# Two weight sums of the first seven-for-eight pair made early, and a second load buffer for up's second tiles

## The chip, the cores and the metric

One Trainium2 chip, of which the kernel uses one core. The core's engines are TensorE (PE; its weight loads are listed as PEld), VectorE (DVE), ScalarE (ACT), GpSimd (POOL) and SyncE (SP), which here only issues DMA transfers. The metric is the device time of one execution in microseconds (us), as the median of several runs.

## The reference

One layer of a hybrid decoder for 512 prompt tokens and 32 sample tokens (T = 544 columns), all in float32: a half-step FFN, a token mixer (differential attention beside an mLSTM), and a second half-step FFN. Only the two FFNs bear on the change:

```python
def half_ffn(x, g_pre, g_post, w_gate, w_up, w_down):
    h = rmsnorm(x, g_pre)
    u = jax.nn.silu(h @ w_gate) * (h @ w_up)
    return x + 0.5 * rmsnorm(u @ w_down, g_post)
```

`w_gate` and `w_up` are 1024 x 2816, `w_down` is 2816 x 1024. The FFN dimension is cut into KF = 22 tiles of 128, the model dimension into KT = 8 blocks of 128 (WK = 4 is half of them), and the columns into two halves of HALF = 272.

## The kernel before

**Precision.** A float32 product is made of three matmuls in a faster float format: each operand is split into a high and a low part, and high x high, high x low and low x high are added in PSUM. `parts` makes a split: ScalarE casts the high part (L240), VectorE subtracts it from the source (L241). Weight splits land in tiles `wh` and `wl`, three of each, and a new one waits until an old one's last matmul.

**Phases of an FFN.** `ffn` runs twice (li = 0, then li = 1 after the mixer).

1. *Plain tiles*, m = 0 to 3 (PLAIN = 4). For each tile and column half, `gate` and `upper` are 24 matmuls each (L252 to L254). The norm's factor `rstd` isn't applied to the input but to the result, by VectorE on reading PSUM (L561 for gate, L575 for up); so the first products can run before the sums of squares are ready. Tiles 0 and 1 are written out at the head of `ffn`, and `lead_out` reads out the first results once `rstd` is there. Tiles 2 and 3 are a list of eight jobs (`jobs`), of which the last three are left for later (`beside`).
2. *Seven-for-eight pairs*, m = 4 to 21, two at a time. Strassen's scheme: the model dimension is halved and the columns are halved, and seven products instead of eight are made of sums of weight blocks and sums of input blocks. The input sums ("factors", tiles `t` and `h8`) are made once by the generator `right_parts`: VectorE scales X (L423), combines quarters and splits each. The weight sums are made by `quadrants` for each pair. With g0, g1 and u0, u1 the upper and lower halves of gate's and up's weights, product 7 uses s3 = g0 + u0, product 5 uses u0 + u1, product 6 adds g0 to that, and product 3 adds g1. All four sums are VectorE adds of 128 x 1024 (L490, the helper `plus`). In order, the products are 1, 5, 6, 2, 7, 3, 4; each is 2 x 12 matmuls (L474 to L476). During the first pair, the rest of the factors and the three left jobs are made between the products.
3. *The down projection*, `down`.

**Weights.** SP loads them. `ffn_weights` yields the split plain tiles gate 0, up 0, gate 1, up 1 and so on; one load of 1 MB holds two neighbouring tiles. For m = 0 and 1 the two buffers of pool `raw` are loaded by `ffn_first`; for m = 2 and 3 gate's and up's loads take the same two buffers again, as they become free (L225). The pairs' weights come through the inner function `raws` (L648): the first pair's gate half lies in the not yet used part of tile `u`, its up half in tile `rawx`.

**Space.** Pools are stacked. In the first FFN, the pool `early` with tile `xt` (six blocks of 4 KB per partition) holds the input rows; after the transposes `bias_windows` uses block 0 (`oh`), block 1 (`rb`) and block 2 (`gsb`) for a small matmul (L961), a copy (L962) and a DMA out (L964). The pool of the `t` factors, three tiles of 8.5 KB, opened after that, begins where `early` began. In the second FFN it lies on tiles of the mixer that hold the last w_out weights (`wt2`). The pool `h8` has four tiles; the factors for products 2, 7, 3 and 4 take one each. The sum s3 lies in the first half of `X0`.

**Order.** The kernel is written against a layer that tracks which instruction uses which bytes, chooses among the ready instructions of an engine by planned times at build, and fixes the resulting order for each engine; a tile that is asked for while all buffers of its pool are in use waits. During the setup in the first FFN, TensorE's order is the written one, up to and with the matmul at L961. Each engine and each DMA queue takes its instructions in the fixed order.

Of the kernel before, what the change touches and what calls it, by code (L numbers as in the profile page):

```python
# [10 lines left out]
F32 = mybir.dt.float32  # L11
# [3 lines left out]
ALU = mybir.AluOpType  # L15
# [19 lines left out]
KT = D // 128  # L35
KF = FFN // 128
# [3 lines left out]
WK = 4  # L40
# [3 lines left out]
PLAIN = 4  # L44
# [160 lines left out]
class _Builder:  # L205
# [188 lines left out]

    def ffn_weights(self, li, first=None, skip=0):

        wg, wu, _ = self.ffn_views(li)
        for mc in range(KF // 2):
            cs = slice(mc * 256, mc * 256 + 256)
            if mc == 0:  # L400
                rg, ru = first or self.ffn_first(li)
            else:
                rg, ru = self.load_raw(wg[:, :, cs], 256), self.load_raw(wu[:, :, cs], 256)
            for sub in range(2):
                for r in (rg, ru):
                    if skip:
                        skip -= 1
                    else:
                        yield self.split(r, KT, sub * 128, step=KT)
# [66 lines left out]
            self.last_mm = nc.tensor.matmul(ps, lhsT=wl[:, k, cs], rhs=high, start=False, stop=sp,  # L476
                                            skip_group_check=True).ins

    def quadrants(self, loaded, raws, small, kept, put, beside, making):

        nc = self.nc
        flat = self.X.tiles[0].rearrange("p k t -> p (k t)")
        s3 = flat[:, 0:1024].rearrange("p (k m) -> p k m", k=WK)
        space = flat[:, 1024:1024 + 2 * T].rearrange("p (a t) -> p a t", a=2)
        C0, C1 = slice(0, HALF), slice(HALF, T)

        def plus(out, x, y):
            nc.vector.tensor_tensor(out=out, in0=x, in1=y, op=ALU.add)  # L490
        for u in range(PLAIN, KF, 2):
            (g0, g1), (u0, u1) = ((r[:, 0:WK], r[:, WK:KT]) for r in loaded)
            if PLAIN < u < KF - 2:
                loaded = raws(u + 2)
            uu = kept(u) if u < KEEP else space
            p1, p5, u2 = (small.tile([128, 2, HALF], F32, name=name) for name in ("p1", "p5", "u2"))
            a, b = [], []
            for p in PRODUCTS:
                if u == PLAIN:
                    next(making, None)  # L500
                    if p == 5:
                        loaded = raws(u + 2)

                if p == 5:
                    plus(s3, g0, u0)
                    plus(u0, u0, u1)
                elif p == 6:
                    plus(u0, u0, g0)
                elif p == 3:
                    plus(u0, u0, g1)  # L510
                src = {1: g0, 2: g1, 4: u1, 7: s3}.get(p, u0)
                w = [x.rearrange("p (k a) m -> p k (a m)", a=2) for x in self.w_tiles()]
                self.parts(src, *w)
                for r in range(2):
                    if p == 1:
                        a.append(self.acc.tile([128, 512], F32, name="acc")[:, 0:HALF])
                    elif p == 5:
                        b.append(self.ps_tile()[:, 0:HALF])
                    ps = b[r] if p in (5, 3) else self.smp.tile([128, 512], F32, name="smp")[:, 0:HALF] if p == 2 else a[r]
                    self.seven(ps, p, w, slice(r * 128, r * 128 + 128), p in (1, 5, 2), p in (2, 3, 4))  # L520
                    if p in (1, 5, 6):
                        nc.scalar.copy(out={1: p1, 5: p5, 6: u2}[p][:, r], in_=ps)
                    elif p == 2:
                        x = uu[:, r, C0]
                        plus(x, ps, p1[:, r])
                        nc.scalar.activation(out=x, in_=x, func=AF.Silu, scale=-1.0)
                    elif p == 7:
                        plus(uu[:, r, C1], ps, p5[:, r])
                    elif p == 3:
                        x = u2[:, r]  # L530
                        plus(x, ps, x)
                        nc.scalar.activation(out=x, in_=x, func=AF.Silu, scale=-1.0)
                    elif p == 4:
                        x = uu[:, r, C0]
                        nc.vector.tensor_tensor(out=x, in0=ps, in1=x, op=ALU.mult)
                    if u == PLAIN:
                        next(beside, None)
                if p == 3:
                    x = uu[:, :, C1]
                    nc.vector.tensor_tensor(out=x, in0=x, in1=u2, op=ALU.mult)  # L540
            if u >= KEEP:
                put(u, uu)

    def ffn(self, li, hs, ws, gpre, gpost, finish, before=None, u=None, lead=None, done=None):

        nc, tc = self.nc, self.tc
# [3 lines left out]
        def weight():  # L550
            return ready.pop(0) if ready else next(gen)
        with ExitStack() as ctx:
# [43 lines left out]
            if not lead:  # L596
                first = [self.mmh(p, x, hs, 0) for p, x in zip((pg, pu, pn), w)]
# [30 lines left out]
            xd = tc.dram_tile([128, KT, T], F32, name="x_ffn%d" % li)  # L628
            for k in range(0, KT, WK):
                nc.gpsimd.dma_start(out=xd[:, k:k + WK], in_=self.X[:, k:k + WK])  # L630
            factors = ctx.enter_context(tc.tile_pool(name="t%d" % li, bufs=3))

            place = own.tile([128, 2 * OWN, T], F32, name="u")
            making = self.right_parts(gpre, place, factors)
            more = tc.tile_pool(name="more%d" % li, bufs=1)
            small = more.__enter__()
            views = self.ffn_views(li)

            def raws(m):
                if m == PLAIN:  # L640
                    g = place[:, KT:2 * OWN].rearrange("p k t -> p (k t)")[:, 0:2048].rearrange("p (k m) -> p k m", k=KT)
                else:
                    g = self.raw.tile([128, 8, 256], F32, name="raw")
                u = self.X.tiles[1].rearrange("p k t -> p (k t)")[:, 0:2048].rearrange("p (k m) -> p k m", k=KT)
                if (m - PLAIN) % 4 == 0:
                    u = small.tile([128, 8, 256], F32, name="rawx")
                for r, w in zip((g, u), views):
                    nc.sync.dma_start(out=r, in_=w[:, :, m * 128:m * 128 + 256])  # L648
                return g, u
# [6 lines left out]
            for i, (f, m, half) in enumerate(jobs[:last]):  # L656
                if i % 4 == 0:
                    w = {gate: weight(), upper: weight()}
                if i == 0:
                    first = raws(PLAIN)  # L660
                f(m, half, w[f])
                upto = max(0, steps * (i + 1 - ahead) // (last - ahead))
                for _ in range(done, upto):
                    next(making)
                done = upto

            def beside():
                for f, m, half in jobs[last:]:
                    f(m, half, w[f])
                    yield  # L670
# [9 lines left out]
            def put(m, uu):  # L680
# [3 lines left out]
                s = self.own[:, i:i + 4].rearrange("p (a b) t -> p a b t", a=2)  # L684
                self.parts(uu, s[:, 0], s[:, 1])
                rows.update({m + a: (s[:, 0, a, :], s[:, 1, a, :]) for a in range(2)})
            self.quadrants(first, raws, small, kept, put, beside(), making)
            more.__exit__(None, None, None)
            self.down(li, ns, rows, factors, ctx.enter_context(tc.tile_pool(name="late%d" % li, bufs=2)), xd, gpost,
                      finish)  # L690
# [1292 lines left out]
```

## Time and profile before

| what | value |
|---|---|
| median of three runs (lowest to highest) | 1110.11 us (1108.96 to 1114.35) |
| the profiled execution, its own time | 1109.74 us |
| its span in the profile | 1107.9 us |
| mean granted TensorE clock | 0.999 |
| VectorE, ScalarE busy | 858.5 us, 641.0 us |
| DMA moved | 160.35 MB |

The profile is one execution on the chip. Its page gives the busy time of each engine, the span in 40 slices, the chain of work that ended last and the costliest groups of instructions. The trace behind it answers narrower questions: the timeline of an engine in a stretch (start, duration, engine, line, operation, what is written and read, how many rows were joined, and in brackets the idle time just before and what ended it), sums over stretches, who waited for whom (in total, how often, longest), and DMA issues with their time to landing. A tile's name stands without its number, so `acc` is any of three PSUM tiles.

The first FFN takes about the first 370 us, the second about the last 370; the plain tiles give way to the first pair at some 60 us and 767 us.

### The profile page before, as it was taken

The numbers are of one execution on the slowest core, as the hardware profiler recorded it, in microseconds if no ns is written. First come the engines' busy times: TensorE is split into PE (matmuls) and PEld (weight loads), VectorE is DVE, ScalarE is ACT, GpSimd is POOL, SyncE is SP. The second block draws the span as 40 slices with busy tenths as digits, with TensorE's granted clock in tenths as the row PEclk, the third lists the DMA queues.
The fourth block names the chain that finished last, engine by engine and source line by source line (L and its number), as shares of the span: only waits on it lengthen the run. The fifth ranks groups of instructions, "written<-read, shape, count | busy, mean of one in ns | idle before, by whom it ended". The sixth has DMA issues, their size and how long they took to land. (4 is left out here: it accounts for less than half of the span.)

```text
span 1107.9 us, 21556 instructions
## 1 busy us (share of the span) xinstructions
PE 1087.6 (98%) x8616; PEld 1048.7 (95%) x8616; DVE 858.5 (77%) x1636; ACT 641.0 (58%) x1292; POOL 155.1 (14%) x201
## 2 busy tenths in 40 slices
PE   8999999999999999999999999999999999999997
PEld 7999999999999998889889879999999999999997
DVE  5898787888577899658776477899987778957764
ACT  4655454565557657667564566774555455555664
POOL 0100000000110234421243541000000000012000
PEclk9999999999999999999999999999999999999999
DMA  9534233326995244643355645765233323299822
GB/s 262 192 123 148 77 114 94 98 83 190 225 221 182 65 142 136 197 125 91 86 165 173 180 143 184 212 212 173 90 97 97 112 79 104 68 273 208 187 98 82
DMA packets 145589, 160.35 MB, mean 145 GB/s; under 512 B 6013, under 2 KB 135397, under 8 KB 144208
## 3 DMA queue, kind: packets, MB, share of 16 engines
q1 hardware_dynamic: 115040, 99.11, 29.8%
q0 software_dynamic: 27472, 57.14, 21.0%
q10 hardware_dynamic: 2976, 2.71, 0.9%
q8 instruction: 68, 1.11, 0.4%
q14 instruction: 33, 0.27, 0.1%
HBM read 143.19 MB, written 16.28 MB: 144 GB/s over the span
## 5 line engine op out<-in xcount | busy, mean ns | idle before, releaser
L240 ACT CAST wh<-raw 128x512 fp32r<-128x512 f32 (+2 forms) x169 | 130.9, 800 | 100.8 <-PE acc L253 29.4
L241 DVE TENSOR_TENSOR wl<-raw,wh 128x512 fp32r<-128x512 f32 (+2 forms) x169 | 151.9, 912 | 46.7 <-ACT wh L240 46.0
L252 PE MATMUL acc<-h,wh 128*128 128x272 f32 x552 | 164.7, 298 | 0.0
L254 PE MATMUL acc<-h,wl 128*128 128x272 f32 x552 | 160.2, 291 | 0.0
L253 PE MATMUL acc<-h,wh 128*128 128x272 f32 x552 | 159.9, 290 | 0.0
L476 PE MATMUL acc<-t,wl 128*128 128x272 f32 x472 | 136.7, 290 | 1.4 <-DVE wl L241 1.4
L474 PE MATMUL acc<-t,wh 128*128 128x272 f32 x472 | 136.7, 290 | 0.0
L475 PE MATMUL acc<-t,wh 128*128 128x272 f32 x472 | 136.1, 289 | 0.0
L252 PEld LDWEIGHTS acc<-h,wh 128*128 128x128 f32 x552 | 104.0, 188 | 8.1 <-issue 7.5
L253 PEld LDWEIGHTS acc<-h,wh 128*128 128x128 f32 x552 | 104.1, 189 | 0.3 <-DVE y L1446 0.2
L254 PEld LDWEIGHTS acc<-h,wl 128*128 128x128 f32 x552 | 103.8, 188 | 0.6 <-issue 0.4
L474 PE MATMUL acc<-h,wh 128*128 128x272 f32 x360 | 104.2, 290 | 0.0
L476 PE MATMUL acc<-h,wl 128*128 128x272 f32 x360 | 104.2, 289 | 0.0
L475 PE MATMUL acc<-h,wh 128*128 128x272 f32 x360 | 103.6, 288 | 0.0
L241 DVE TENSOR_TENSOR wl<-X,wh 128x1024 fp32r<-128x1024 f32 x66 | 80.7, 1223 | 27.8 <-ACT wh L240 27.7
L240 ACT CAST wh<-X 128x1024 fp32r<-128x1024 f32 x66 | 69.3, 1050 | 40.7 <-PE aux L475 25.9
L476 PEld LDWEIGHTS acc<-t,wl 128*128 128x128 f32 x472 | 88.7, 188 | 1.8 <-DVE wl L241 1.7
L475 PEld LDWEIGHTS acc<-t,wh 128*128 128x128 f32 x472 | 89.0, 189 | 0.1
L474 PEld LDWEIGHTS acc<-t,wh 128*128 128x128 f32 x472 | 88.8, 188 | 0.0
L721 POOL DMA_DIRECT2D late<-in_ffn_w_down_dram x12 | 18.7, 1562 | 438.2 <-issue 376.4
L476 PE MATMUL aux<-h,wl 128*128 128x272 f32 x240 | 69.6, 290 | 0.0
L474 PE MATMUL aux<-h,wh 128*128 128x272 f32 x240 | 69.5, 289 | 0.0
(516 smaller groups left out, 3278.0 us busy)
## 6 DMA issues: line engine op xcount, KB each, us to landing
raw<-in_ffn_w_gate_dram SPq DMA_DIRECT2D x18, 1024.0 KB, 5.4
raw<-in_w_in_dram SPq DMA_DIRECT2D x28, 512.0 KB, 4.4
late<-in_ffn_w_down_dram POOLq DMA_DIRECT2D x12, 1024.0 KB, 9.9
rawx<-in_ffn_w_up_dram SPq DMA_DIRECT2D x10, 1024.0 KB, 5.5
X<-in_ffn_w_up_dram SPq DMA_DIRECT2D x8, 1024.0 KB, 5.5
raw<-in_ffn_w_down_dram SPq DMA_DIRECT2D x8, 1024.0 KB, 9.9
raw<-in_ffn_w_down_dram SPq DMA_DIRECT2D x10, 768.0 KB, 4.8
raw<-in_w_out_dram SPq DMA_DIRECT2D x7, 1024.0 KB, 5.5
```

The lines of the kernel that those rows point to most:

```text
L240: self.nc.scalar.copy(out=high, in_=src)
L241: self.nc.vector.tensor_tensor(out=low, in0=src, in1=high.bitcast(F32), op=ALU.subtract)
L252: nc.tensor.matmul(ps, lhsT=wh, rhs=xh(k0 + k), start=st, stop=False)
L253: nc.tensor.matmul(ps, lhsT=wh, rhs=xl(k0 + k), start=False, stop=False)
L254: self.last_mm = nc.tensor.matmul(ps, lhsT=wl, rhs=xh(k0 + k), start=False, stop=sp).ins
L474: nc.tensor.matmul(ps, lhsT=wh[:, k, cs], rhs=high, start=st, stop=False, skip_group_check=True)
L475: nc.tensor.matmul(ps, lhsT=wh[:, k, cs], rhs=low, start=False, stop=False, skip_group_check=True)
L476: self.last_mm = nc.tensor.matmul(ps, lhsT=wl[:, k, cs], rhs=high, start=False, stop=sp, skip_group_check=True).ins
L721: nc.gpsimd.dma_start(out=ts[j], in_=rows_of(a, j, up), accum_op=ALU.add)
```

## The change

Three edits, all in the two FFNs:

- **The first pair's two sums.** s3 = g0 + u0 and u0 + u1 of the first pair (m = 4) are written right after the pair's loads, before the first of the jobs of tiles 2 and 3, no longer inside `quadrants` at product 5. The first one's result lies in a tile of `h8` instead of `X0`. Later pairs make their sums as before.
- **Up's second tiles.** The load of up's tiles 2 and 3 goes into a tile of the pool of `t` factors (`self.spare`), no longer into the second buffer of `raw`.
- The loop of `ffn_weights` ends after the plain tiles; nothing asked for later ones.

```diff
     def ffn_weights(self, li, first=None, skip=0):
         wg, wu, _ = self.ffn_views(li)
-        for mc in range(KF // 2):
+        for mc in range(PLAIN // 2):
             cs = slice(mc * 256, mc * 256 + 256)
             if mc == 0:
                 rg, ru = first or self.ffn_first(li)
             else:
-                rg, ru = self.load_raw(wg[:, :, cs], 256), self.load_raw(wu[:, :, cs], 256)
+                rg = self.load_raw(wg[:, :, cs], 256)
+                ru = self.spare.tile([128, 8, 256], F32, name="t")
+                self.nc.sync.dma_start(out=ru, in_=wu[:, :, cs])
...
-    def quadrants(self, loaded, raws, small, kept, put, beside, making):
+    def quadrants(self, loaded, s3, raws, small, kept, put, beside, making):
...
         flat = self.X.tiles[0].rearrange("p k t -> p (k t)")
-        s3 = flat[:, 0:1024].rearrange("p (k m) -> p k m", k=WK)
...
-                if p == 5:
+                if p == 5 and u > PLAIN:
+                    s3 = flat[:, 0:1024].rearrange("p (k m) -> p k m", k=WK)
                     plus(s3, g0, u0)
                     plus(u0, u0, u1)
...
-            factors = ctx.enter_context(tc.tile_pool(name="t%d" % li, bufs=3))
+            self.spare = factors = ctx.enter_context(tc.tile_pool(name="t%d" % li, bufs=3))
...
                 if i == 0:
                     first = raws(PLAIN)
+                    s3 = self.h8.tile([128, WK, 256], F32, name="h8")
+                    for out, x in ((s3, first[0]), (first[1][:, 0:WK], first[1][:, WK:KT])):
+                        nc.vector.tensor_tensor(out=out, in0=x[:, 0:WK] if x is first[0] else x, in1=first[1][:, 0:WK],
+                                                op=ALU.add)
...
-            self.quadrants(first, raws, small, kept, put, beside(), making)
+            self.quadrants(first, s3, raws, small, kept, put, beside(), making)
```

## The prediction

> **What bounds the kernel now.** The page comes first: its span line and the line of busy times.
>
> ```profile
> span 1107.9 us, 21556 instructions
> PE 1087.6 (98%) x8616; PEld 1048.7 (95%) x8616; DVE 858.5 (77%) x1636; ACT 641.0 (58%) x1292; POOL 155.1 (14%) x201
> ```
>
> TensorE is busy for 1087.6 of 1107.9 us, so 20.3 us is all that any change can win that takes no matmul away, and this one takes none away. The profiled execution took 1109.74 us, 1.84 more than its span; the median of the three runs is 1110.11, so I work from 1109.74 and keep 0.4 us in mind. Next, the table of stretches around the first pair in each FFN (each stretch, its length, then busy time and instructions of PE, PEld, DVE, ACT, POOL, then clock, DMA share and GB/s).
>
> ```profile
> 20.00:46.00 26.00, 26.00 (x191) 23.87 (x190) 21.13 (x49) 18.93 (x42) 2.18 (x4) 1.00 0.72 242
> 46.00:91.00 45.00, 44.58 (x350) 43.99 (x350) 44.77 (x57) 22.63 (x31) 5.07 (x10) 1.00 0.49 153
> 744.00:769.00 25.00, 23.89 (x188) 23.59 (x187) 23.21 (x35) 14.62 (x22) 3.24 (x6) 1.00 0.55 177
> 769.00:800.00 31.00, 30.21 (x236) 29.91 (x237) 29.96 (x36) 15.49 (x23) 1.62 (x3) 1.00 0.41 134
> ```
>
> In the first FFN VectorE has 4.87 us to spare from 20 to 46 us and 0.23 from 46 to 91: there it is full. TensorE nevertheless loses only 0.42 there. In the second FFN TensorE loses 1.11 + 0.79 = 1.90 between 744 and 800, beside a VectorE that is idle for 1.79 and 1.04. So what can be won near the edit is 0.42 + 1.90 = 2.3 us. The waits of TensorE in these places, the first FFN's first:
>
> ```profile
> PE acc L252 <- DVE sqe L575: 0.4, 1, 0.4
> ```
> ```profile
> PE acc L476 <- DVE wl L241: 1.4, 1, 1.4
> PE acc L252 <- DVE sq L561: 0.4, 1, 0.4
> ```
>
> Three waits, all on VectorE: two for a PSUM tile that it reads out late, one for the low half of the first product's weights.
>
> **The change, part by part.** *The two sums.* VectorE's rows of the first pair, first FFN and then second:
>
> ```profile
> 64.04 1.20 DVE L490 TENSOR_TENSOR X<-u,rawx 128x1024 f32<-128x1024 f32 x1
> 65.17 1.27 DVE L241 TENSOR_TENSOR t<-u,t 128x1088 fp32r<-128x1088 f32 x1
> 66.37 0.42 DVE L575 TENSOR_TENSOR sqe<-acc,r 128x272 f32<-128x272 f32 x1
> 66.72 1.20 DVE L490 TENSOR_TENSOR rawx<-rawx 128x1024 f32<-128x1024 f32 x1
> ```
> ```profile
> 768.06 1.22 DVE L241 TENSOR_TENSOR wl<-u,wh 128x1024 fp32r<-128x1024 f32 x1
> 771.95 1.23 DVE L490 TENSOR_TENSOR X<-u,rawx 128x1024 f32<-128x1024 f32 x1
> 774.63 1.22 DVE L490 TENSOR_TENSOR rawx<-rawx 128x1024 f32<-128x1024 f32 x1
> ```
>
> The sums are these two L490 adds. Their count, size and operand memories stay; only their place moves, so 2 x 1.20 = 2.4 us of VectorE per FFN go from the full stretch to an earlier one. In the first FFN the reader at 66.37, for which TensorE waited 0.4, stands behind the 1.20 at 64.04: without it, it comes earlier than it is needed. What is late next is nothing that the waits show, so **-0.4**. In the second FFN the reader of the third wait comes after 774.63, behind both adds: **-0.4**. The wait of 1.4 ended with the split at 768.06, ahead of both old adds, so their removal does nothing for it.
>
> What the adds meet in their new place: they need the pair's weights. Issue and landing of `rawx`, first FFN and second:
>
> ```profile
> 21.42 0.58 SPq L648 DMA_DIRECT2D rawx<-in_ffn_w_up_dram  x1
> ```
> ```profile
> rawx<-in_ffn_w_up_dram SPq DMA_DIRECT2D x1, 1024.0 KB, 11.6
> ```
> ```profile
> 730.61 0.37 SPq L225 DMA_DIRECT2D raw<-in_ffn_w_gate_dram  x1
> 738.31 0.37 SPq L648 DMA_DIRECT2D rawx<-in_ffn_w_up_dram  x1
> 745.34 0.37 SPq L225 DMA_DIRECT2D raw<-in_ffn_w_up_dram  x1
> ```
> ```profile
> rawx<-in_ffn_w_up_dram SPq DMA_DIRECT2D x1, 1024.0 KB, 10.3
> ```
>
> First FFN: 21.42 + 11.6 = 33.0 us, ahead of the VectorE idle time in which the sums would fit:
>
> ```profile
> 40.27 0.79 DVE L567 TENSOR_TENSOR sq<-sq,sqe 128x272 f32<-128x272 f32 x2 [1.32 <-ACT sqe L566]
> ```
>
> One 1.20 fits into these 1.32; the other has room among the rest of the 4.87 idle us. Cost 0; if that cover were gone, at most 2 x 1.20 lands on the weight splits of that stretch. Second FFN: 738.31 + 10.3 = 748.6. The sums can't start before that, and from there VectorE is nearly full. Its one long gap:
>
> ```profile
> 752.88 1.22 DVE L241 TENSOR_TENSOR wl<-raw,wh 128x1024 fp32r<-128x1024 f32 x1 [1.49 <-ACT wh L240]
> ```
> ```profile
> 751.79 2.00 ACT L240 CAST wh<-raw 128x1024 fp32r<-128x1024 f32 x2 [2.27 <-DMA raw<-in_ffn_w_up_dram]
> ```
>
> That gap is a wait for up's second tile, issued at 745.34. With the tile in its new place the load needs no `raw` buffer and can go right behind the gate's at 730.61 (the buffer's former holder, the last w_out weights, is read by then), so the gap closes: VectorE has 2.4 us more to do before 769 and 1.49 us less to wait. The balance, +0.95, would fall on the 1.4 wait; at the other end, if the planner leaves the sums until after the split at 768.06, the closed gap takes that wait away. Range -1.45 to +0.95, taken as **0**, near the middle, since nothing tells the order.
>
> ```profile
> 738.53 0.55 POOL L630 DMA_DIRECT2D x_ffn<-X  x1 [4.08 <-DVE X L363]
> ```
>
> `rawx` took 10.3 us beside this save of X from another queue, against 5.5 for the load at 36.41 below. [...]
>
> *Up's second tile in the first FFN.* The new place is the first buffer of pool `t`, which lies where `early` was: its 8 KB per partition are blocks 0 and 1 of `xt`, which the bias windows use for `oh` and `rb` until their matmul at L961 (`gsb` lies in block 2). Rows of the old load and its split, and of TensorE:
>
> ```profile
> 36.41 0.37 SPq L225 DMA_DIRECT2D raw<-in_ffn_w_up_dram  x1
> ```
> ```profile
> raw<-in_ffn_w_up_dram SPq DMA_DIRECT2D x1, 1024.0 KB, 5.5
> ```
> ```profile
> 43.00 1.23 DVE L241 TENSOR_TENSOR wl<-raw,wh 128x1024 fp32r<-128x1024 f32 x1 [0.19 <-ACT wh L240]
> ```
> ```profile
> 44.09 0.81 PE L961 MATMUL aux<-xt 33*4 33x384 f32 x2
> 44.83 0.40 PE L252 MATMUL acc<-ha,wh 128*128 128x272 f32 x1
> ```
> ```profile
> 44.90:52.70 7.80, 7.80 (x62) 7.80 (x63) 7.80 (x14) 2.61 (x4) 2.89 (x5) 1.00 0.45 120
> ```
>
> The load can be issued at 44.09 + 0.81 = 44.90 instead of 36.41. It lands 5.5 later, 50.40; a cast of 1.0 (two took 2.00 above) and a subtract of 1.23 make the tile ready at 52.63. TensorE spaces its matmuls by 7.80/62 = 0.126 us, 24 to a product: gate of tile 2 runs 44.83 to 47.85, and the next product by the written order is up of tile 2. In that order TensorE would stand still for 52.63 - 47.85 = **4.8 us**. It need not be in that order, for the order on the engines isn't the written one:
>
> ```profile
> 60.19 0.29 PE L475 MATMUL acc<-t,wh 128*128 128x272 f32 x1
> 60.32 0.29 PE L252 MATMUL acc<-ha,wh 128*128 128x272 f32 x1
> ```
>
> `seven` writes its twelve matmuls in one run; here plain ones stand after the second, because the low half wasn't planned to be ready. A planner that knows the load to be late has gate of tile 2 for the other half and gate of tile 3 to put first, 2 x 3.02 us, which reaches 53.9 and covers 52.63. Between 0 and +4.8 I take **0**; the planner fixes the order before the run, so a load later than planned still stalls. On SP, later loads stand behind this one's wait. The next one before was this:
>
> ```profile
> 50.98 6.35 SPq L648 DMA_DIRECT2D raw<-in_ffn_w_gate_dram  x2
> ```
>
> It comes after 44.90, so nobody is late by that.
>
> *The factor's place.* The sum's `h8` tile is the fourth factor's buffer, so factor 4 must wait until product 7's weights are split off the sum:
>
> ```profile
> 78.92 1.22 DVE L241 TENSOR_TENSOR wl<-X,wh 128x1024 fp32r<-128x1024 f32 x1
> ```
> ```profile
> 79.04 1.11 ACT L240 CAST h<-u 128x1088 fp32r<-128x1088 f32 x1 [0.60 <-DVE u L448]
> ```
> ```profile
> 88.44 0.29 PE L474 MATMUL acc<-h,wh 128*128 128x272 f32 x1
> ```
>
> Split done at 80.14, cast 1.11, subtract 1.27: 82.5, and product 4 begins at 88.44. Nothing, with 5.9 us of cover; were the cover gone, the 1.1 us by which the cast moves. Likewise the third `t` factor now shares its place with up's tile, split before that factor is made. The shortened range of `ffn_weights` costs nothing, since nobody asked it for later tiles.
>
> **Sum.** -0.4 - 0.4 + 0 + 0 = -0.8: 1109.74 - 0.8 = 1108.9, and with half of the 0.4 by which the median lies higher, **1109.1 us**.
>
> **The rivals.** *Sums wait for their weights (second FFN).* If the planner believes `rawx` to land at the usual time, about 5.5 us after 738.31, it puts the sums at some 744 us, and VectorE, which works in order, stands until 748.6. Behind them stand the read-outs of PSUM and the splits; 2.4 us of sums then follow, and what VectorE lacks by 769 grows from 0.95 to some 3. For it: it stood 1.49 us at 752.88 for just such a misjudged load. Against it: the products ahead of the pair have some us of lead. Place 1111: 1109.74 - 0.8 + 0.95 to 3.
>
> *Up's tile late (first FFN), the slower side.* TensorE in the old order at 47.85 waits until 52.63: 1109.74 + 4.8 - 0.8 = 1113.7. It decides as soon as fewer than two other products (6.0 us) are put ahead. If the tile's place is kept until `gsb` is out as well, the load starts at 48.99 at the earliest:
>
> ```profile
> 48.99 0.74 POOL L967 DMA_DIRECT2D windows<-bias_row  x1 [1.29 <-DMA bias_row<-xt]
> ```
>
> 48.99 + 5.5 + 2.23 = 56.7, a stall of 8.9, and 1117.8. For it: the load moves from 8 us ahead of need to behind it. Against it: the planner's freedom above.
>
> *The edit doesn't do what it says.* The adds may be planned later than rstd's wait, where they were; then only up's tile has moved: 1109 to 1110. Or a new plan shifts waits elsewhere, in the 20.3 us of idle time, by one or two us either way. All three waits gone at once gives 1109.74 - 2.3 = 1107.4, the best that the rows hold.
>
> **How the numbers follow.** Forecast (1107.4 to 1110): 0.45. Sums wait (1110 to 1112.5): 0.27. Up's tile late (1112.5 to 1118): 0.15. Another plan: 0.13, of which 0.04 is a win over 0.5% from places that I can't name. About 0.5%, 5.5 us, is what a measurement of this kernel can tell from no change: below 1104.6 is faster, above 1115.7 slower. So faster 0.04; slower 0.10, most of the late-tile cases and a few of another plan; same 0.86. The range 1106.0 to 1114.6 leaves out the far part of the late tile and of another plan, about 0.17 together.
>
> **What would show it.** Right: the two L490 adds stand before 46 us and before 760; TensorE has no idle row between 46 and 91; the wait at L575 is gone. Sums wait: a VectorE row of L490 (or the new line) idle on DMA `rawx`, near 748. Late tile: TensorE idle at 47 to 57 us with ScalarE's cast behind DMA up. Factor 4 wrong: TensorE idle ahead of product 4. A change of TensorE's time outside 30 to 95 and 730 to 800 would mean a new plan, and my sum wouldn't explain it.

## The result, and the profile after

The changed kernel takes **1123.01 us** (median of six runs, 1119.45 to 1125.01), the kernel before beside it 1111.37 (six runs, 1108.96 to 1114.35): ratio 1.0105, 95% interval [1.0087, 1.0124]. It is slower by about 11.7 us, and outside the predicted range. The profiled execution took 1119.66 us, 9.92 more than the profiled one of before.

The first lines of the changed kernel's page:

```profile
span 1117.8 us, 21558 instructions
PE 1089.6 (97%) x8616; PEld 1051.0 (94%) x8616; DVE 860.3 (77%) x1636; ACT 640.6 (57%) x1292; POOL 155.8 (14%) x201
```

The matmuls are as many as before (8616), and TensorE is busy for 2.0 us more, though it has nothing more to do. The idle time is 28.2 us, where it was 20.3. So two things have to be found: about 8 us of new idle time, and 2 us by which the same matmuls have become longer. TensorE's waits in the changed kernel answer the first (what it waited for, us in total, times, longest):

```profile
PE acc L252 <- ACT wh L240: 7.1, 1, 7.1
PE aux L254 <- DVE wl L241: 3.5, 1, 3.5
...
PE acc L252 <- DVE sqe L579: 0.2, 1, 0.2
```

The waits of 1.4, 0.4 and 0.4 that the prediction quoted are gone or halved (L575 is now L579). In their place stand two long ones, each once.

**The first, 7.1 us, in the first FFN.** The load of up's second tile on SP's queue, the bias windows' transfers on GpSimd's, the cast on ScalarE, and TensorE, all of the changed kernel:

```profile
46.08 0.37 SPq L406 DMA_DIRECT2D t<-in_ffn_w_up_dram  x1
```
```profile
44.25 0.52 POOL L972 DMA_DIRECT2D bias_row<-xt  x1 [0.89 <-DVE xt L970]
44.77 0.56 POOL L581 DMA_DIRECT2D u_keep<-sqe  x1
46.51 0.74 POOL L975 DMA_DIRECT2D windows<-bias_row  x1 [1.18 <-DMA bias_row<-xt]
```
```profile
42.58 0.80 PE L969 MATMUL aux<-xt 33*4 33x384 f32 x2
...
46.32 0.29 PE L254 MATMUL acc<-ha,wl 128*128 128x272 f32 x1
53.70 0.60 PE L252 MATMUL acc<-ha,wh 128*128 128x272 f32 x1 [7.10 <-ACT wh L240]
```
```profile
51.61 1.10 ACT L240 CAST t<-u 128x1088 fp32r<-128x1088 f32 x1
52.61 1.04 ACT L240 CAST wh<-t 128x1024 fp32r<-128x1024 f32 x1
```

The load went out at 36.41 before and goes out at 46.08 now. The bias matmul (L969, once L961), whose operands lie where the load writes, ended at 43.38, so that is not what the load waited for. It goes out when `bias_row`, the transfer that reads `gsb`, is done (issued at 44.25, 1.7 us to landing); `windows`, which waits for the same transfer, follows at 46.51. From 46.08 the rest is serial: 5.4 us to land, a place behind a factor's cast that began at 51.61, then the tile's own cast. TensorE's last row before ends at 46.6, and its next is up of tile 2: nothing was put between.

**The second, 3.5 us, in the second FFN.** VectorE in the changed kernel, then TensorE:

```profile
749.76 0.43 DVE L565 TENSOR_TENSOR sq<-smp,r 128x272 f32<-128x272 f32 x1
753.83 1.23 DVE L667 TENSOR_TENSOR h<-u,rawx 128x1024 f32<-128x1024 f32 x1 [3.64 <-DMA rawx<-in_ffn_w_up_dram]
754.97 1.22 DVE L241 TENSOR_TENSOR wl<-raw,wh 128x1024 fp32r<-128x1024 f32 x1
```
```profile
756.24 0.40 PE L254 MATMUL aux<-ha,wl 128*128 128x272 f32 x1 [3.53 <-DVE wl L241]
```

The early sum (L667) stands at the head of VectorE's queue and waits 3.64 us for `rawx`. Right behind it stands the low half of up's tile 1, which TensorE needs. (In the changed kernel the second FFN runs 6.5 us later than before, by the first FFN's excess; its times are to be read against that.)

**The matmuls that became longer.** The table of stretches of the changed kernel, cut at the places where the granted clock changes (it is the column ahead of the last two):

```profile
53.70:57.00 3.30, 3.29 (x14) 3.19 (x15) 3.30 (x4) 2.90 (x3) 0.00 (x0) 0.50 0.64 222
57.00:60.00 3.00, 3.00 (x25) 3.00 (x24) 3.00 (x4) 0.00 (x0) 0.00 (x0) 0.96 0.79 244
...
756.70:760.10 3.40, 3.40 (x18) 3.40 (x17) 3.40 (x6) 0.20 (x1) 0.54 (x1) 0.54 0.76 240
760.10:763.00 2.90, 2.90 (x24) 2.90 (x23) 2.62 (x6) 0.66 (x2) 0.00 (x0) 0.95 0.38 128
```

Behind each of the two waits TensorE runs at half its clock for some 3.5 us: 14 and 18 matmuls in 3.3 and 3.4 us, where the next stretches of some 3 us have 25 and 24. By the records the half clock lasts until 57.24 in the first place, and from 756.97 to 760.39 in the second (the 0.96 and 0.95 of the next stretches are its ends). Half of 3.54 and 3.41 us is lost, an estimate of 1.8 and 1.7.

**The ledger.** I count TensorE's matmuls (8616 in every run here) and compare when the same ones start. Numbers 150 to 500 span the plain tiles and the beginning of the first pair in the first FFN, numbers 5600 to 6150 the same of the second. All in us, from the traces:

| run | 150 to 500 | against before | 5600 to 6150 | against before |
|---|---|---|---|---|
| before | 46.31 | | 72.50 | |
| changed | 54.29 | +7.98 | 76.11 | +3.61 |
| e1, sums alone | 45.65 | -0.66 | 77.12 | +4.62 |
| e2, tile alone | 54.44 | +8.13 | 70.93 | -1.57 |
| e3, `gsb` moved | 55.32 | +9.01 | 77.87 | +5.37 |
| e4, bias windows moved | 46.98 | +0.67 | 77.99 | +5.49 |
| e5, gates first | 53.01 | +6.70 | 77.23 | +4.73 |
| e6, one edit in each FFN | 45.65 | -0.66 | 70.91 | -1.59 |
| e7, first FFN's sums alone | 45.64 | -0.67 | 72.52 | +0.02 |
| e8, e6 with second sums held back | 45.65 | -0.66 | 70.16 | -2.34 |

The two stretches of the changed kernel account for 7.98 + 3.61 = 11.59; outside them it was 1.7 faster in the profiled execution (9.92 in all), 1.5 of it in the setup ahead of matmul 150, which the edit does not touch. Of the 11.59, 8.6 is idle and 3.0 busy time of TensorE; elsewhere it was busy for 1.0 less, so the page shows 2.0.

The ledger compares single executions, and that of before, with 1109.74 us, lies 3.1 us under the median of the 17 runs beside which the first experiments stand. The sums of its two stretches agree within 2 us with the excesses measured by ratio, but not for e4: 6.16 for a measured 2.7. That difference is open.

### The profile page after: what moved, and what is told of

Read it like the earlier page. It is cut to its first block, busy times and chain, and to the rows that moved or that the text cites. A ratio compares the mean times of both kernels' runs of the same rounds, so it can differ in the third digit from the quotient of the medians.

```text
span 1117.8 us, 21558 instructions
## 1 busy us (share of the span) xinstructions
PE 1089.6 (97%) x8616; PEld 1051.0 (94%) x8616; DVE 860.3 (77%) x1636; ACT 640.6 (57%) x1292; POOL 155.8 (14%) x201
## 4 chain that ended last, share of the span: by engine, by line
PE 82%; DVE 9%; DMA 4%; ACT 3%; issue 1%; POOL 0%; POOLq 0%; ACTq 0%; SPq 0%; DVEq 0%
PE acc L479 9%; PE acc L477 9%; PE acc L478 9%; PE acc L252 6%; PE acc L254 6%; PE acc L253 6%; PE aux L479 5%; PE aux L477 5%; PE aux L478 5%; PE smp L479 2%; PE smp L477 2%; PE smp L478 2%; DVE wl L241 2%; PE smp L1381 1%; PE acc L744 1%
## 5 line engine op out<-in xcount | busy, mean ns | idle before, releaser
L240 ACT CAST wh<-raw 128x512 fp32r<-128x512 f32 (+2 forms) x165 | 126.8, 794 | 97.2 <-PE acc L253 33.5
L241 DVE TENSOR_TENSOR wl<-raw,wh 128x512 fp32r<-128x512 f32 (+2 forms) x165 | 146.9, 904 | 43.3 <-ACT wh L240 42.6
L241 DVE TENSOR_TENSOR wl<-X,wh 128x1024 fp32r<-128x1024 f32 x64 | 78.3, 1223 | 30.0 <-ACT wh L240 30.0
```

The source lines that it names most:

```text
L240: self.nc.scalar.copy(out=high, in_=src)
L241: self.nc.vector.tensor_tensor(out=low, in0=src, in1=high.bitcast(F32), op=ALU.subtract)
```

## The experiments

The theory: two separate stalls. One comes of the place that up's second tile was given in the first FFN, the other of the early sum's place in VectorE's order in the second; behind each the clock falls. The rivals: a transfer that delays another, a stall that needs both edits, and sums that cost wherever they stand. Ratios are to the kernel before, run beside each: 1112.83 us in the median, 17 runs for e1 to e4 and 29 for e6 to e8.

**e1: the sums without the tile.** Up's second tiles are loaded into `raw` again.

```diff
-                rg = self.load_raw(wg[:, :, cs], 256)
-                ru = self.spare.tile([128, 8, 256], F32, name="t")
-                self.nc.sync.dma_start(out=ru, in_=wu[:, :, cs])
+                rg, ru = self.load_raw(wg[:, :, cs], 256), self.load_raw(wu[:, :, cs], 256)
```

> The changed kernel with up's second tiles loaded into raw again, as before; the two sums stay in their early place in both FFNs. Theory A (two separate stalls: the first FFN's 7.10 us comes from the place of up's second tile alone, the second FFN's 3.53 us from the early sum alone, which stands on VectorE ahead of a split and waits for rawx): no TensorE idle row at 47 to 57 us, the row of about 3.5 us near 756 stays, with a half clock record behind it; 2 to 3.5 us over the kernel before. Theory B (rawx lands late because up's second tile is now ahead of it in the second FFN and takes its share of the transfers): rawx lands by 750, no row at 756, 0.5 to 2 us under the kernel before. Theory C (the early sums also cost the first FFN something): a row of idle time on TensorE between 30 and 57 us that the kernel before does not have.

Measured: 1116.13 us, ratio 1.0048 [1.0029, 1.0067], about 5.3 us over before. TensorE's waits between 725 and 800 us, SP's load of `rawx` and VectorE's wait for it:

```profile
PE aux L254 <- DVE wl L241: 4.8, 1, 4.8
```
```profile
738.36 0.37 SPq L650 DMA_DIRECT2D rawx<-in_ffn_w_up_dram  x1
750.99 0.37 SPq L225 DMA_DIRECT2D raw<-in_ffn_w_up_dram  x1
```
```profile
748.60 1.22 DVE L665 TENSOR_TENSOR h<-u,rawx 128x1024 f32<-128x1024 f32 x1 [4.86 <-DMA rawx<-in_ffn_w_up_dram]
```

Theory A: the first FFN has no stall and is 0.66 shorter; the second has its stall. Theory B falls: here up's second tile is loaded behind `rawx` (750.99), and `rawx` still takes from 738.36 to 748.60, as before the change (738.31, 10.3 us). The excess is larger than the 2 to 3.5 expected. By the ledger 3.96 us of it lie in the two stretches, where the wait is longer than in the changed kernel (4.8 for 3.5); what the rest comes of is open.

**e2: the tile without the sums.** The sums are made at product 5, as before.

```diff
-                if p == 5 and u > PLAIN:
+                if p == 5:
...
-                    s3 = self.h8.tile([128, WK, 256], F32, name="h8")
-                    for out, x in ((s3, first[0]), (first[1][:, 0:WK], first[1][:, WK:KT])):
-                        nc.vector.tensor_tensor(...)
+                    s3 = None
```

> The changed kernel with the two sums back in the wait for the rstd, in factor 4's place, as before; up's second tiles still load into a t in both FFNs. Theory A (two separate stalls): the row of about 7.1 us at 53.7 stays with its half clock, and the second FFN has no row of 3.5 us at 756 but the waits of the kernel before (1.45 and 0.45 us); 7.5 to 9 us over the kernel before. Theory B (the two edits make the stalls only together, through the order or through the transfers): at least one of the two rows is gone from here and from the run with the sums alone, and the excesses of the two runs do not add up to the 11.6 us between the two kernels.

Measured: 1118.54 us, 1.0061 [1.0043, 1.0079], 6.8 over before. TensorE's waits between 20 and 100 us, and between 725 and 800:

```profile
PE acc L252 <- ACT wh L240: 6.9, 1, 6.9
```
```profile
PE acc L252 <- DVE sq L565: 0.4, 1, 0.4
```

Theory A again, with one thing that it did not expect, and that puts the excess under the 7.5 to 9 expected: the second FFN is not like before but 1.57 shorter, its wait of 1.4 gone. The excesses of e1 and e2 add up, 0.48% + 0.61% = 1.09% for the 1.05% of both together, so neither stall needs the other edit.

**e3: what holds the place.** `gsb` goes to block 5 of `xt`, which the load does not overwrite.

```diff
-        oh, rb, gsb = space[0:r, 0, 0:w], space[0:r, 1, 0:H], space[0:H, 2, 0:w]
+        oh, rb, gsb = space[0:r, 0, 0:w], space[0:r, 1, 0:H], space[0:H, 5, 0:w]
```

> The changed kernel with the copy gsb of the bias windows put into block 5 of xt instead of block 2, beyond the 8 KB per partition that the t of up's second tile covers. Theory A (the place comes free as a whole: the load waits for the last reader of any part of xt, the store of gsb): the load is issued at 46 us as in the changed kernel, TensorE's idle row stays at 7.1 us, and the time is that of the changed kernel within 0.5%. Theory B (the load waits only for what it overwrites, oh and rb, whose last reader is the bias matmul that ends at 43.4): the load is issued near 43.5, the idle row is 4.5 us, and the time falls by 2.5 to 3 us.

Measured: 1128.1 us, 1.0133 [1.0104, 1.0161]. The load on SP's queue, and the stall on TensorE:

```profile
46.49 0.37 SPq L406 DMA_DIRECT2D t<-in_ffn_w_up_dram  x1
```
```profile
54.12 0.59 PE L252 MATMUL acc<-ha,wh 128*128 128x272 f32 x1 [7.10 <-ACT wh L240]
```

Theory A: nothing comes earlier. The place is given back as a whole, when the last reader of any part of `xt` is done. The ratio lies 0.3% above the changed kernel's, and the two intervals overlap; in the profiled executions the half clock lasts longer behind the waits (5.9 and 5.2 us here, 3.5 and 3.4 there), and the second FFN's wait is 4.5 for 3.5.

**e4: `xt` out of the way.** The bias windows work in an `h8` tile of their own.

```diff
-        self.bias_windows(xt)
+        self.bias_windows(self.h8.tile([128, 3, 384], F32, name="h8"))
```

> The changed kernel with the bias windows' three small blocks in an h8 of their own instead of in xt; all else as changed. Theory A (the first FFN's stall is only the late issue of up's second tile, held up by the use of xt for the bias windows): the load is issued before 40 us, no TensorE idle row stands at 47 to 57 us, the granted clock is full there, and the time is 8 to 9 us under that of the changed kernel, 2 to 3.5 us over the kernel before; the second FFN's row of 3.5 us is untouched. Theory B (the load is late whatever becomes of xt, by the queue or by the transfers beside it): a row of at least 3 us stays near 53 us.

Measured: 1115.97 us, 1.0024 [1.0005, 1.0043], 2.7 over before. SP's load, TensorE's waits between 20 and 100 us, and the one in the second FFN:

```profile
24.92 0.37 SPq L406 DMA_DIRECT2D t<-in_ffn_w_up_dram  x1
```
```profile
PE acc L479 <- DVE wl L241: 0.8, 1, 0.8
```
```profile
750.96 0.59 PE L254 MATMUL aux<-ha,wl 128*128 128x272 f32 x1 [4.47 <-DVE wl L241]
```

Theory A: the load goes out 21 us earlier and the 7.1 us are gone. With e3 this closes the first stall: the lifetime of `xt`, no queue and no traffic. The row of 0.8 is new, a wait of the first seven-for-eight product at 60.02; this first FFN is 1.3 us longer than e1's. Why is open.

**e5: is the order on TensorE free?** Both gate halves of a tile are written ahead of the up halves.

```diff
-            jobs = [(f, m, half) for m in range(2, PLAIN) for half in range(2) for f in (gate, upper)]
+            jobs = [(f, m, half) for m in range(2, PLAIN) for f in (gate, upper) for half in range(2)]
```

> The changed kernel with the jobs of tiles 2 and 3 in the order gate half 0, gate half 1, up half 0, up half 1 instead of gate, up, gate, up for each half, so that two products of gate's tile stand ahead of the first product with up's tile 2. Theory A (the first FFN's stall stands because the order on TensorE is fixed ahead and has one product of about 3 us between the last work that is ready and the late tile): the load of up's second tile is issued at 46 us as in the changed kernel, and TensorE's idle row of 7.1 us shrinks by the one product that comes in ahead, to 4 to 4.5 us; the row of the second FFN stays between 3.5 and 4.8 us. Theory B (the order on TensorE follows the loads, so the order in the program does not matter): the row stays at 7 us.

Measured: one run, 1121.89 us. The load, TensorE, and the stretch behind the wait:

```profile
46.15 0.37 SPq L406 DMA_DIRECT2D t<-in_ffn_w_up_dram  x1
```
```profile
53.50 0.40 PE L252 MATMUL acc<-ha,wh 128*128 128x272 f32 x1 [3.81 <-ACT wh L240]
...
55.79 0.60 PE L254 MATMUL acc<-ha,wl 128*128 128x272 f32 x1 [0.51 <-DVE wl L241]
```
```profile
53.60:60.50 6.90, 6.39 (x27) 5.76 (x28) 5.60 (x5) 5.84 (x6) 0.00 (x0) 0.52 0.81 253
```

Theory A: one product more of written lead takes 3.3 us off the wait, so the order follows the program here and not the load. Yet the stretch became only 1.28 shorter (6.70 for 7.98): the whole half-clock stretch of 6.8 us now lies behind the first wait (53.91 to 60.74), with the second wait of 0.51 in it, and the clock costs about 3.2 by the same estimate (half of 6.32), where the changed kernel lost 1.8. The second FFN's wait is 4.7 us, within what was expected.

**e6 and e7: the halves that cost nothing.** e7 is the kernel before with the early sums in the first FFN alone. e6 adds up's second tiles in a `t` in the second FFN alone. Against the changed kernel, e6 is:

```diff
-                ru = self.spare.tile([128, 8, 256], F32, name="t")
+                ru = (self.spare.tile if li else self.raw.tile)([128, 8, 256], F32, name="t" if li else "raw")
...
-                    first = raws(PLAIN)
+                    first, s3 = raws(PLAIN), None
+                if i == 0 and li == 0:
                     s3 = self.h8.tile([128, WK, 256], F32, name="h8")
...
-                if p == 5 and u > PLAIN:
+                if p == 5 and (u > PLAIN or s3 is None):
```

> Each half of the change where no stall came of it: in the first FFN the two early sums, with up's second tiles in raw as before; in the second FFN up's second tiles in a t, with the sums in factor 4's place as before. Theory A (the gains seen in the runs with one half each stay, and the stalls were those of the other places): 0.7 us less in the first FFN between 55 and 75 us and 1.6 us less in the second between 750 and 770 than the kernel before, no TensorE idle row over 1.5 us in either, full clock; 1.5 to 2.5 us under the kernel before. Theory B (these gains are the recovery from the stalls, or scatter between executions): within 0.5 us of the kernel before in both stretches.

> The kernel before with the early sums in the first FFN alone; up's second tiles in raw, the second FFN's sums in factor 4's place. Theory A (the first FFN's gain comes from the sums and the second FFN's from up's second tile in a t): 0.7 us less than the kernel before between 55 and 75 us; between 750 and 770 nothing changes, with the waits of 1.4 and 0.4 us on the seven-product lines there. Theory B (the second FFN's gain does not hang on the tile's place): 750 to 770 is shorter than in the kernel before here too, by over 1 us.

Measured: e6 1112.07 us, 0.9990 [0.9971, 1.0009]; e7 1113.39 us, 1.0010 [0.9990, 1.0030]. TensorE's waits between 725 and 800 us, e6 and then e7:

```profile
PE acc L252 <- DVE sq L565: 0.4, 1, 0.4
```
```profile
PE acc L479 <- DVE wl L241: 1.5, 1, 1.5
PE acc L252 <- DVE sq L565: 0.4, 1, 0.4
```

Theory A for both by the ledger: the first FFN is 0.66 shorter in each, and the second 1.59 shorter only where the tile has its new place. It is not recovery from a stall, as there was none. On the whole time neither can be told from the kernel before: of the 1.5 to 2.5 us expected of e6 the medians show 0.8.

**e8: the second FFN's sums, early but not first.** As e6, but in the second FFN too the sums are made ahead of product 5, into X's first tile, and so behind the scalings that read it.

```diff
-                    first, s3 = raws(PLAIN), None
-                if i == 0 and li == 0:
-                    s3 = self.h8.tile([128, WK, 256], F32, name="h8")
+                    first = raws(PLAIN)
+                if i == (0, 3)[li]:
+                    s3 = (self.X.tiles[0].rearrange("p k t -> p (k t)")[:, 0:1024].rearrange("p (k m) -> p k m", k=WK)
+                          if li else self.h8.tile([128, WK, 256], F32, name="h8"))
...
-                if p == 5 and (u > PLAIN or s3 is None):
+                if p == 5 and u > PLAIN:
```

> As the run with each half where no stall came of it, and besides the second FFN's two sums are made ahead of product 5 after all, but into X's first tile, which keeps them behind the four scalings that read that tile and so behind the splits of up's second tiles. Theory A (the second FFN's stall was the place in VectorE's order, ahead of a split, and not the sums themselves): no row near 750, and the stretch from 750 to 790 is as short as in the run without early sums there, or shorter by up to 0.5 us; 1.5 to 2.5 us under the kernel before. Theory B (early sums in the second FFN cost wherever they stand, because VectorE is full there): a TensorE idle row of 1 us or more on a plain or seven-product line between 750 and 790, and no gain over the kernel before in that stretch.

Measured: 1111.70 us, 0.9988 [0.9971, 1.0005]. VectorE, and then one row of the stretch table for e8 and one for the kernel before:

```profile
748.46 1.22 DVE L241 TENSOR_TENSOR wl<-t,wh 128x1024 fp32r<-128x1024 f32 x1
...
755.18 1.21 DVE L669 TENSOR_TENSOR X<-u,rawx 128x1024 f32<-128x1024 f32 x1
```
```profile
744.00:800.00 56.00, 56.00 (x444) 55.79 (x442) 54.52 (x74) 31.04 (x46) 4.88 (x9) 1.00 0.42 141
```
```profile
744.00:800.00 56.00, 54.11 (x424) 53.50 (x424) 53.17 (x70) 30.11 (x45) 4.86 (x9) 1.00 0.47 153
```

Theory A: the sums themselves cost nothing there. With the splits ahead of them TensorE has no idle time at all in these 56 us, and the ledger shows 2.34 us less, 0.75 of it over e6, where at most 0.5 had been expected. Both FFNs together are 3.0 us shorter than before. That is 0.27%; the medians differ by 1.1 us, where 1.5 to 2.5 had been expected, and the interval still holds 1: e8 beats the changed kernel clearly, and the kernel before not measurably.

## Why the prediction was wrong

- **"Up's second tile in the first FFN", taken as 0: the step that failed first.** It was excused by "a planner that knows the load to be late", which would put two other products ahead. The plan put none ahead (46.32 to 53.70 on TensorE), and e5 shows that the order moves when the program does. The prediction also had the place free once the bias matmul was done and kept the other case, `gsb` out first, only as an afterthought with a stall of 8.9. That one is what happens (e3, e4), with 7.1 for 8.9: `windows` was issued at 46.51 for 48.99, and the first matmul needs the cast alone and not the subtract, while TensorE came to the tile 1.2 us earlier (46.6 for 47.85) and the tile's cast stood behind a factor's. Its argument that the load moved "from 8 us ahead of need" also counted too much: the old load landed at 41.9 (36.41 + 5.5) for a product at 47.85, so some 6 us ahead.
- **The second FFN's balance, taken as 0: the other step that failed.** What happened is the first rival, by its own mechanism: the sum is planned before the load lands, VectorE stands until then. Its landing time, 748.6, is what e1 shows (748.60). Two of its parts were wrong. The price, "+0.95 to 3", counted the work that VectorE lacks later; but the wait passes to TensorE at once, since the low half of up's tile 1 stands behind the sum (3.53, and 4.8 in e1). And the argument against it, that the products ahead of the pair have some us of lead, looked at the pair, when the instruction behind the sum served a plain tile.
- **The clock: not in the sum.** +1.8 and +1.7 us behind the waits, by the estimate above. The trace of before held no case that showed it: its wait of 1.45 us at 769.34 was followed by a granted clock of 1.00 (769 to 800). In the changed kernel's trace the half-clock stretches at the two waits are 6.83 us long (50.41 to 57.24) and 3.41 (756.97 to 760.39). From which length on a wait brings one is not shown: a half clock followed a wait of 1.77 us in e7, and none followed one of 1.79 in the kernel before (last section).
- **The rivals were priced one by one.** They sit in two FFNs and add up. With the prices that the prediction had for them, 1109.74 - 0.8 + 8.9 + 3 = 1120.8, and with 4.8 for 8.9 it is 1116.7; the range ended at 1114.6.
- **-0.4 in the first FFN: right**, and a bit more, -0.66 (e1, e6, e7, e8). Their new place costs nothing there, as predicted: 32.09 and 34.79 in the changed kernel.
- **-0.4 in the second FFN and the closed gap: right, where no stall hides them.** -0.75 for the sums' removal from the full stretch (e8 against e6), and -1.59 for the tile's earlier load (e6 against before), just past the end of -1.45 that the prediction gave it.
- **A delay of `rawx` by up's tile ahead of it** (theory B of e1): no run shows it, and none tests it. In the changed kernel up's tile went out at 733.00 and took 5.3 us, so it had landed before `rawx` went out at 744.76. `rawx` took 9.0 us there and 10.2 with up's tile behind it (e1).
- **The factor's place, 0: right.** No wait stands ahead of product 4 in any run.

## What to carry to other kernels

When work is moved earlier on an engine that runs in order, look at what stands directly behind it there: if its input can be late, that neighbour is late too (VectorE's 3.64 us for `rawx` became 3.53 of TensorE's), and the mean idle time of the engine says nothing about it; a dependency that holds the moved work behind the urgent work (e8) keeps the gain of that stretch without the stall. When a load is given the place of something else, find the last reader of that place, a transfer out included, and compare it with the time at which the load used to start; don't count on a plan made at build to step around a late load. Price the cases that can happen together as a sum, and add to each wait of TensorE the half-clock time that can follow it (2.96 to 6.32 us behind the waits of 3.5 to 7.1 us here).

## What the runs showed of the hardware

Each wait of TensorE below cost more than its length, and how much more differs from run to run: the half clock behind it lasted 2.96 to 6.32 us. By the records of the granted clock in the changed kernel, up to the program's end, the half-clock stretches are 6.83 and 3.41 us long, and the full-clock stretches ahead of and between them 44.37 and 699.73 (13 and 205 times 3.413); one is 6.83 in e5 too (53.91 to 60.74). An estimate of the cost of a wait is its length and half of what remains of the half-clock stretch when TensorE starts again, or half of the whole stretch where that begins only later (the changed kernel's second: TensorE starts at 756.24, the stretch at 756.97). It comes within 0.4 us of the ledger in each row:

| run, stretch | wait | half clock after it | sum of wait and half of that | growth of the ledger across the wait |
|---|---|---|---|---|
| changed, first FFN | 7.10 | 3.54 | 8.87 | 9.0 |
| e2, first | 6.94 | 4.73 | 9.30 | 9.3 |
| e3, first | 7.10 | 5.86 | 10.03 | 10.0 |
| e5, first | 3.81 + 0.51 | 6.32 | 7.48 | 7.8 |
| changed, second FFN | 3.53 | 3.41 | 5.24 | 5.3 |
| e1, second | 4.76 | 2.96 | 6.24 | 6.3 |
| e3, second | 4.52 | 5.18 | 7.12 | 7.1 |
| e4, second | 4.47 | 5.53 | 7.24 | 7.2 |
| e5, second | 4.73 | 5.16 | 7.31 | 7.3 |

In e5 the second wait of the first FFN falls into the half-clock stretch of 6.83 and is taken off it. The last column compares the starts of the same matmuls, ahead of the wait and behind the half-clock stretch, with those of before. A wait of 4.47 (e4) cost 7.2 us, more than one of 4.76 (e1) with 6.3.

The half clock followed shorter waits as well, and not each time. In the mixer of e7 TensorE waits 1.77 us for VectorE (until 567.13), and the half clock follows from 567.63 to 571.04. In the kernel before TensorE waits 1.79 us in the setup (until 17.45), 1.38 at 395.27 and 1.45 at 769.34, and none follows: the granted clock is 1.00 from 7.26 to 1106.35, and the last matmul ends at 1101.2. In the second FFN's later part of e8's profiled execution it followed two waits close together; TensorE's rows and the stretch table:

```profile
990.85 0.40 PE L744 MATMUL acc<-u,wh 128*128 128x272 f32 x1 [1.16 <-ACT wh L240]
...
991.84 0.39 PE L746 MATMUL acc<-u,wl 128*128 128x272 f32 x1 [0.47 <-DVE wl L241]
```
```profile
988.00:992.00 4.00, 2.36 (x17) 1.92 (x16) 1.11 (x2) 2.04 (x4) 0.00 (x0) 1.00 1.20 219
992.00:995.40 3.40, 3.40 (x17) 3.40 (x18) 0.80 (x1) 0.23 (x2) 0.00 (x0) 0.54 1.14 275
```

The kernel before had no such wait there in its profiled execution. What comes behind matmul 6150 took 314.2 us in e8 and 310.9 in the kernel before, more than e8 wins in the two stretches. That may be a part of why executions of one kernel differ by some us here; the runs do not settle it, as only one execution of each has a trace.
